# Raw weights in half tiles, another DMA rate in the planner, and one pool for block inverses and attention values, in a two-layer hybrid trunk

## The chip, the cores and the metric

The kernel runs on one core of one Trainium2 chip. The metric is device time in microseconds (us) of one execution. Names used below: PE is TensorE (matmuls), PEld its weight loads, DVE is VectorE, ACT is ScalarE, POOL is GpSimd, SP is SyncE, whose queue issues nearly all DMAs.

## The reference, cut to what matters

The input x is 512 tokens by 1024 channels; all numbers are fp32. Head width is 128. Layer 0 mixes with four gated DeltaNet heads (short convolution, chunked delta rule with chunks of 64) and four block-sparse MoBA heads; layer 1 has eight forgetting-attention (FoX) heads. Each mixer is `(mix * silu(z)) @ w_out`. After each layer comes a gate from the residual stream times a projection of a per-layer embedding p (256 wide).

```python
def ab_mixer(hn, w_in, ...):
    proj = hn @ w_in                       # 1024 x 4104
    ...                                    # conv, silu, l2norm; delta rule; MoBA
    y = jnp.concatenate([from_heads(oa), from_heads(ob)], axis=-1) * jax.nn.silu(z)
    return y @ w_out

def fox_mixer(hn, w_in, forget_b, w_out):
    proj = hn @ w_in                       # 1024 x 4104
    ...                                    # causal softmax(q.k/sqrt(d) + c_t - c_s)
    return (from_heads(o) * jax.nn.silu(z)) @ w_out

def reference(x, p, ...):
    for i in range(DEPTH):
        j = i // 2
        hn = rmsnorm(x, norm_g[i])
        if i % 2 == 0: x = x + ab_mixer(hn, w_in_ab[j], ...)
        else:          x = x + fox_mixer(hn, w_in_c[j], ...)
        gate = jax.nn.sigmoid(rmsnorm(x, ple_norm_g[i]) @ w_ple_gate[i])
        x = x + gate * (p[i] @ w_ple_proj[i])
    return rmsnorm(x, final_g)
```

In the delta rule a unit lower-triangular system is solved in each chunk of 64 tokens: `sol = triangular_solve(eye + a_mat, rhs)`, with `u, w = sol[..., :dv], sol[..., dv:]`.

## The kernel before, in words

**Weights.** Every weight product is made of three matmuls: each fp32 weight chunk `raw` is split on the chip into `whi` (a copy in the matmul's type) and `wlo = raw - whi`; activations are split into `hhi`, `hlo` (or `yhi`, `ylo`) likewise; hi·hi, lo·hi and hi·lo are summed in PSUM. The class `Weights` (L445 on) does it for all of `w_in`, `w_out`, `w_ple_gate` and `w_ple_proj`. A piece is 1024 x 512 weights, 2 MB, in one SBUF tile `raw` of 16 KB in each partition; two DMAs of 1 MB fill it. There is one such tile: the pair of DMAs for the next piece is issued when the last split of this piece has read it. A piece has four chunks. A chunk made by `cols` is 128 columns over all eight row blocks, so it reads both halves of the piece; a chunk made by `rows` is two row blocks of 512 columns and reads one half. Of split chunks there are three slots each (`whi`, `wlo`). A split is one copy of 128x1024 (`whi`, on ACT or DVE) and one subtraction of 128x1024 (`wlo`, on DVE or POOL). In the product `u` a chunk feeds 24 matmuls of 128x512; `vr` is the same with the weights as the moving side.

**The order.** A planner (`Plan`, L123 to L325) runs when the kernel is built. It keeps a clock for every engine, gives each operation a cost, and writes one fixed order of instructions for each engine and for the DMA queue of SP. It puts an operation next where its inputs are ready by its own clocks. All operations pass L186, so each row of the profile has that line; tiles tell them apart. A DMA's time in it is set on L177, by bytes:

```python
self.bw = max(end + 0.7, self.bw) + max(b / 1e6 * 2.8, ...) ...
```

The hardware then follows the written order: each engine takes its instructions one after the other, and waits in front of the one whose inputs aren't there, whatever stands behind it. Where the planner's own clock has PE waiting for 0.2 us, it puts a matmul named `idle` in PE's order (`until`, L291), which computes nothing that is used.

**Tiles.** `t2` has 55 slots of 2 KB in each partition, `t4` four of 4 KB. Two further tiles of 8 KB, `bd`, hold first the projection weights of the first embedding (`ple0`) and gate weights, later the inverses of the 64x64 blocks (`bds`) of the delta rule, one tile for the inverse and one for its transpose, each for all four heads. The inverses are worked out on DVE (`inverses`, L1156), written to DRAM (`xd`) and read back in block-diagonal form by eight DMAs of 64 KB on SP; the flag `bds` then lets `wy` (L1188) go on, which reads `wq` from DRAM and gives PE the products `t`, `w` and `u` of each head. Loads of weights are held from the start of the inverses' last part until these eight DMAs are issued (`Wait` in `loads`).

**Attention.** For 128 queries: `S` on PE, bias, maximum and exponent on DVE and ACT (`P`), transposes on PE (`PTp`), split into `PThi`, `PTlo` on ACT and DVE, and `O` on PE. In the FoX layer these stand in the engines' orders among the weight splits of the products beside them. FoX values are split into `vhi`, `vlo`.

## Time and profile before

| | |
|---|---|
| median of 3 runs | 742.52 us (739.96 to 742.71) |
| the profiled execution | 739.63 us, of which its span is 737.9 |
| PE busy | 702.7 us, 95% of the span, 3374 matmuls |
| DVE, ACT, POOL busy | 474.7, 341.1, 279.8 us (64, 46, 38%) |
| mean granted clock of PE | 0.986 |
| HBM read, written | 68.53 MB, 11.30 MB; 108 GB/s over the span |

A matmul's recorded time is longer than its share of PE: matmuls overlap, and their ends are modelled, so PE's time is best counted from start to start. The timeline has 96 matmuls `u` of 128x512 in a row in 22.10 us, 0.230 us each. Idle time in front of an instruction is shown with what ended it; the view of the waits sums it by engine and by what was waited for. The granted clock of a window (PEclk) is near 1.00 at 2.4 GHz and near 0.50 at 1.2 GHz. A transfer of DMA is read from its issue on SP's queue to the first instruction that waited for it.

### The profile page before, as it was taken

The page shows a single profiled execution, that of the slowest core. Times are in us where ns is not written, and L with a number is a line of the kernel's source. Part 1 is how long each engine was busy: PE and PEld are TensorE (multiplying, and loading weights), DVE is VectorE, ACT ScalarE, POOL GpSimd, SP SyncE. Part 2 cuts the span into 40 slices and gives each one's busy share as a digit, 9 for nine tenths or more (in the row PEclk, how much of TensorE's full clock was granted, in tenths as well). Part 3 has the DMA queues.
Part 4 walks back from the last instruction along what each step waited for, and adds up shares of the span by engine and source line. Part 5 has one row for each costly group of instructions (what it writes and reads, how often), then busy time and mean ns, then how long its engine had stood idle before and what let it go on. Part 6 is the DMA issues. An engine that isn't in the chain of part 4 may idle for free.

```text
span 737.9 us, 9199 instructions
## 1 busy us (share of the span) xinstructions
PE 702.7 (95%) x3374; PEld 577.9 (78%) x3374; DVE 474.7 (64%) x805; ACT 341.1 (46%) x634; POOL 279.8 (38%) x222
## 2 busy tenths in 40 slices
PE   7999988999999999999998999989999799999995
PEld 4887876888788787778886888868888688888884
DVE  3768864966665678776896443546337466776684
ACT  4638842225774364634553422345224463433545
POOL 3435554426551223025322344342336322535320
PEclk9999999999999999999999999989999999999998
DMA  7752424443424023143554035310453203244303
GB/s 257 261 144 78 152 73 128 143 114 90 111 58 115 2 69 116 25 165 125 200 185 125 17 116 141 96 49 1 114 143 100 72 1 138 79 170 157 114 1 114
DMA packets 51782, 80.41 MB, mean 109 GB/s; under 512 B 11133, under 2 KB 14542, under 8 KB 51738
## 3 DMA queue, kind: packets, MB, share of 16 engines
q1 hardware_dynamic: 51064, 78.74, 34.5%
q10 hardware_dynamic: 674, 1.09, 0.5%
q8 instruction: 26, 0.43, 0.2%
q14 instruction: 18, 0.15, 0.1%
HBM read 68.53 MB, written 11.30 MB: 108 GB/s over the span
## 4 chain that ended last, share of the span: by engine, by line
PE 69%; DMA 13%; DVE 9%; ACT 3%; POOL 3%; issue 2%; SPq 1%; ACTq 0%; DVEq 0%; POOLq 0%
PE u L186 40%; PE vr L186 8%; DMA raw<-in_w_in_c_dram 6%; DMA raw<-in_w_in_ab_dram 4%; PE O L186 3%; PE pp L186 3%; PE fg L186 3%; POOL wlo L186 2%; PE S L186 2%; ACT whi L186 2%; PE PTp L186 2%; DVE gt L186 1%; DVE wlo L186 1%; DMA bd<-in_w_ple_proj_dram 1%; PE su L186 1%
## 5 line engine op out<-in xcount | busy, mean ns | idle before, releaser
L186 POOL TENSOR_TENSOR wlo<-raw,whi 128x1024 fp32r<-128x1024 f32 x74 | 186.5, 2526 | 360.0 <-ACT whi L186 280.6
L186 PE MATMUL u<-hhi,whi 128*128 128x512 f32 x480 | 190.7, 397 | 3.2 <-ACT whi L186 3.1
L186 PE MATMUL u<-hlo,whi 128*128 128x512 f32 x480 | 190.2, 396 | 0.0
L186 PE MATMUL u<-hhi,wlo 128*128 128x512 f32 x480 | 163.1, 397 | 0.1
L186 ACT ACTIVATE whi<-raw 128x1024 fp32r<-128x1024 f32 x84 | 87.3, 1054 | 117.7 <-DMA raw<-in_w_in_c_dram 49.5
L186 PEld LDWEIGHTS u<-hhi,whi 128*128 128x128 f32 x480 | 90.3, 188 | 22.1 <-ACT whi L186 3.5
L186 PEld LDWEIGHTS u<-hhi,wlo 128*128 128x128 f32 x480 | 89.7, 188 | 18.4 <-POOL wlo L186 0.6
L186 PEld LDWEIGHTS u<-hlo,whi 128*128 128x128 f32 x480 | 90.3, 188 | 17.3
L186 DVE TENSOR_TENSOR wlo<-raw,whi 128x1024 fp32r<-128x1024 f32 x20 | 36.9, 1844 | 24.8 <-ACT whi L186 24.8
L186 PE MATMUL u<-yhi,whi 128*128 128x512 f32 x128 | 50.2, 392 | 1.4 <-ACT whi L186 1.4
L186 PE MATMUL vr<-wlo,hhi 128*128 128x512 f32 x128 | 51.4, 401 | 0.0
L186 PE MATMUL vr<-whi,hlo 128*128 128x512 f32 x128 | 51.3, 401 | 0.0
L186 PE MATMUL vr<-whi,hhi 128*128 128x512 f32 x128 | 51.3, 401 | 0.0
L186 PE MATMUL u<-ylo,whi 128*128 128x512 f32 x128 | 50.0, 391 | 0.0
L186 ACT ACT_TABLE_LOAD x33 | 42.3, 1283 | 2.1 <-DVE cacc L186 0.8
L186 PE MATMUL u<-yhi,wlo 128*128 128x512 f32 x128 | 42.4, 391 | 0.7 <-POOL wlo L186 0.7
L186 ACT ACTIVATE hhi<-xres,vec 128x512 fp32r<-128x512 f32 x24 | 17.3, 724 | 44.1 <-DVE xres L186 44.0
L186 ACT ACTIVATE P<-P,nmx 128x128 f32<-128x128 f32 (+3 forms) x48 | 26.7, 557 | 12.6 <-DVE nmx L186 11.7
L186 DVE SCALAR_TENSOR_TENSOR cacc<-u,vec,cacc 128x509 f32<-128x509 f32 (+2 forms) x36 | 26.7, 744 | 7.0 <-ACT cacc L186 6.4
L186 PEld LDWEIGHTS u<-yhi,whi 128*128 128x128 f32 x128 | 24.1, 188 | 6.7 <-ACT whi L186 1.9
L186 PEld LDWEIGHTS u<-yhi,wlo 128*128 128x128 f32 x128 | 24.0, 188 | 6.0 <-POOL wlo L186 1.1
L186 PEld LDWEIGHTS vr<-whi,hlo 128*128 128x128 f32 x128 | 24.6, 193 | 4.9
(299 smaller groups left out, 1277.8 us busy)
## 6 DMA issues: line engine op xcount, KB each, us to landing
raw<-in_w_in_ab_dram SPq DMA_DIRECT2D x16, 1024.0 KB, 9.7
raw<-in_w_in_c_dram SPq DMA_DIRECT2D x16, 1024.0 KB, 7.0
raw<-in_w_ple_gate_dram SPq DMA_DIRECT2D x8, 1024.0 KB, 5.0
raw<-in_w_out_ab_dram SPq DMA_DIRECT2D x4, 1024.0 KB, 7.2
raw<-in_w_out_c_dram SPq DMA_DIRECT2D x4, 1024.0 KB, 6.5
xr<-in_x_dram SPq DMA_DIRECT2D x8, 256.0 KB, 5.6
x0d<-x SPq DMA_DIRECT2D x8, 256.0 KB, 8.0
ppd<-ppt SPq DMA_DIRECT2D x8, 256.0 KB, 4.1
```

Of the source, the lines that this page charges most:

```text
L186: return op.f(*op.a, **op.k)
```

## The change

The tile of 16 KB for raw weights becomes three of 8 KB, each half of a piece, with its own slot, DMA and release. A half is loaded as soon as a slot is free, so that the first half of the next piece can be loaded while the piece before it is still being split. A `cols` chunk, which reads both halves, is split by two copies and two subtractions of 128x512; a `rows` chunk reads one half, and keeps one copy and one subtraction of 128x1024. In the planner, the cost of a DMA goes from 2.8 us for each MB to 5.2 for `w_in` and 3.4 for the rest. The two tiles of 8 KB go, `t4` has eight slots rather than four and `t2` 51 rather than 55. The block inverses are four tiles of 4 KB, for two heads each, filled by 16 DMAs of half the size (128x the same partitions, half the rows), the second pair of tiles only after the inversion; `wy` of heads 0 and 1 waits for the first pair alone (`bds0`). The first embedding's weights are two tiles of `t4`, `vhi`/`vlo` share one, and MoBA's values lie in two. Some tiles near the end are given back earlier.

```diff
@@ -174,7 +174,7 @@
             o = op.outs[0] if op.outs[0].space != bass.MemoryType.DRAM else op.ins[0]
             b = o.nbytes if not callable(o.nbytes) else o.nbytes()
             small = any(n.startswith(("kd", "ub", "xd", "graw", "vrow", "bd_", "qd", "gd", "Gb")) for n in op.w + op.r)
-            self.bw = max(end + 0.7, self.bw) + max(b / 1e6 * 2.8, 0.6 if small else 0.2) + 1.5 * ("graw" in op.w[0])
+            self.bw = max(end + 0.7, self.bw) + max(b / 1e6 * (5.2 if any("w_in" in n for n in op.r) else 3.4), 0.6 if small else 0.2) + 1.5 * ("graw" in op.w[0])
             end = self.bw + 0.9
         if op.locks():
             self.lock = end
...
@@ -322,7 +322,7 @@
         self.until(lambda: not any(g[4] for g in gs), "finish")
-NB2, NBH = 55, 16
+NB2, NBH = 51, 16
 PI = -1.6
...
@@ -353,8 +353,8 @@
         return (wp if pool in ("raw", "whi", "wlo") else gp).tile(shape, dt, name=nm(name), tag=f"{pool}_{i}", bufs=1)
     plan = Plan(make)
-    for pool, n in (("A", 4), ("B", 4), ("t2", NB2), ("th", NBH), ("t4", 4),
-                    ("raw", 1), ("whi", 3), ("wlo", 3)):
+    for pool, n in (("A", 4), ("B", 4), ("t2", NB2), ("th", NBH), ("t4", 8),
+                    ("raw", 3), ("whi", 3), ("wlo", 3)):
         plan.pools(pool, n)
     V, A, G, T, SP = (Eng(k, o) for k, o in (("DVE", nc.vector), ("ACT", nc.scalar), ("POOL", nc.gpsimd),
                                             ("PE", nc.tensor), ("SP", nc.sync)))
...
@@ -393,12 +393,10 @@
-    bd = [gp.tile([P, GH * NT * P], F32, name=nm("bd"), tag="bd", bufs=2)]
-    ple0 = bd[0].rearrange("p (k c) -> p k c", k=2)
+    ple0 = [plan.take("t4", "ple", (P, 2, 512)) for _ in range(2)]
-        do(A.dma_start(ple0[:, :, c * 512:(c + 1) * 512],
-                       w_ple_proj[0, :, c * 512:(c + 1) * 512].rearrange("(k q) c -> q k c", q=P)))
+        do(A.dma_start(ple0[c], w_ple_proj[0, :, c * 512:(c + 1) * 512].rearrange("(k q) c -> q k c", q=P)))
...
@@ -437,10 +435,7 @@
-    def gst_tile():
-        return gp.tile([P, GH * NT, P], F32R, name=nm("gst"), tag="bd", bufs=2)[:, 0:KT, :]
-
-    gst0 = gst_tile()
+    gst0 = plan.take("t4", "gst", (P, KT, P), F32R)
...
@@ -460,15 +455,17 @@
         def cols(self, w, c0):
-            self.add(self.views(w, c0), [(lambda r, j=j: r[:, :, j * P:(j + 1) * P], (KT, P)) for j in range(4)])
+            self.add(self.views(w, c0), [([(h, slice(None), slice(j * P, (j + 1) * P), slice(4 * h, 4 * h + 4)) for h in range(2)],
+                                          (KT, P)) for j in range(4)])
         def rows(self, w, c0):
-            self.add(self.views(w, c0), [(lambda r, j=j: r[:, 2 * j:2 * j + 2, :], (2, 512)) for j in range(4)])
+            self.add(self.views(w, c0), [([(j // 2, slice(2 * (j % 2), 2 * (j % 2) + 2), slice(None), slice(None))], (2, 512))
+                                         for j in range(4)])
         def ple(self, w):
             self.add([w[:, c * 512:(c + 1) * 512].rearrange("(k q) c -> q k c", q=P) for c in range(2)],
-                     [(lambda r, c=c: r[:, 2 * c:2 * c + 2, :], (2, 512)) for c in range(2)])
+                     [([(c, slice(0, 2), slice(None), slice(None))], (2, 512)) for c in range(2)])
         def add(self, views, parts):
             self.pieces.append(views)
...
@@ -480,28 +477,31 @@
                 if views is None:
                     self.loaded.append(ple0)
                     continue
-
-                yield Wait(lambda: "inv3" not in flags or "bds" in flags)
-                raw = yield Slot("raw", "raw", (P, KT, 512))
-                n = views[0].shape[1]
-                for k, view in enumerate(views):
-                    yield SP.dma_start(raw[:, k * n:(k + 1) * n], view)
-                self.loaded.append(raw)
+                self.loaded.append([])
+                for view in views:
+
+                    yield Wait(lambda: "inv3" not in flags or "bds" in flags)
+                    raw = yield Slot("raw", "raw", (P, 4, 512))
+                    yield SP.dma_start(raw[:, 0:view.shape[1]], view)
+                    self.loaded[i].append(raw)
         def splits(self):
-            for i, (piece, f, (a, c)) in enumerate(self.chunks):
-                yield Wait(lambda: len(self.loaded) > piece)
-                raw = f(self.loaded[piece])
+            for i, (piece, parts, (a, c)) in enumerate(self.chunks):
+                yield Wait(lambda: len(self.loaded) > piece and len(self.loaded[piece]) == 2)
+                halves = self.loaded[piece]
                 hi = yield Slot("whi", "whi", (P, a, c), F32R)
                 lo = yield Slot("wlo", "wlo", (P, a, c), F32R)
                 far = i - self.used >= 1
-                yield copy(hi, raw, 0.8)
-                w = [V.tensor_tensor(out=lo, in0=raw, in1=hi.bitcast(F32), op=ALU.subtract),
-                     G.tensor_tensor(out=lo, in0=raw, in1=hi.bitcast(F32), op=ALU.subtract)]
-                yield Any((w[0], 2.5 if far else 0.0), w[1])
+                for h, k, w, o in parts:
+                    yield copy(hi[:, o, :], halves[h][:, k, w], 0.8)
+                for h, k, w, o in parts:
+                    ops = [e.tensor_tensor(out=lo[:, o, :], in0=halves[h][:, k, w], in1=hi[:, o, :].bitcast(F32),
+                                           op=ALU.subtract) for e in (V, G)]
+                    yield Any((ops[0], 2.5 if far else 0.0), ops[1])
                 self.split.append((hi, lo))
-                if piece and (i + 1 == len(self.chunks) or self.chunks[i + 1][0] != piece):
-                    free(raw)
+                rest = {x[0] for q in self.chunks[i + 1:] if q[0] == piece for x in q[1]}
+                for h in {x[0] for x in parts} - rest:
+                    free(halves[h])
                 self.urge()
         def urge(self):
...
@@ -1179,10 +1179,14 @@
         yield V.tensor_copy(vbT, vb.rearrange("p a b -> p b a"))
         yield SP.dma_start(xd[1].rearrange("b h t r c -> (b h t) r c"), vbT)
         drop(vb, vbT)
-        for k in (0, 1):
-            for bl in range(4):
-                yield SP.dma_start(bds[k][bl * 32:(bl + 1) * 32, :, bl * 32:(bl + 1) * 32],
-                                   xd[k, bl].rearrange("h t r c -> r (h t) c"))
+        flags.add("inverted")
+        for h0 in range(2):
+            yield Wait(lambda: len(bds) >= 2 * h0 + 2)
+            for k in (0, 1):
+                for bl in range(4):
+                    yield SP.dma_start(bds[2 * h0 + k][bl * 32:(bl + 1) * 32, :, bl * 32:(bl + 1) * 32],
+                                       xd[k, bl, 2 * h0:2 * h0 + 2].rearrange("h t r c -> r (h t) c"))
+            flags.add(f"bds{h0}")
         flags.add("bds")
     def wy(hh):
...
@@ -1194,10 +1198,10 @@
         yield G.tensor_tensor(out=kdc, in0=kr, in1=b3(eGLG, hh), op=ALU.mult)
         yield G.tensor_tensor(out=kr, in0=kr, in1=b3(eGp, hh), op=ALU.mult)
-        yield flag("bds")
+        yield flag(f"bds{hh // 2}")
         wq = yield Slot("t4", "wq", (P, NT, 4, 64))
         yield SP.dma_start(wq[:, :, 1:3, :], qd[hh].rearrange("p (t c i) -> p t c i", c=2, i=64))
-        bdT, bd = (b[:, hh * NT:(hh + 1) * NT, :] for b in bds)
+        bdT, bd = (b[:, hh % 2 * NT:(hh % 2 + 1) * NT, :] for b in bds[hh // 2 * 2:hh // 2 * 2 + 2])
         ps = yield Slot("B", "t1", (P, NT, P))
         for t in range(NT):
             yield T.matmul(ps[:, t, :], lhsT=kn[hh][:, t * P:(t + 1) * P], rhs=bd[:, t, :], start=True, stop=True)
...
@@ -1310,10 +1316,13 @@
     bds = []
     def blocks():
+
         yield flag("gates")
-        for k in range(2):
-            bds.append(gp.tile([P, GH * NT, P], F32, name=nm("bd"), tag="bd", bufs=2))
-            yield G.memset(bds[k], 0.0)
+        for k in range(4):
+            yield flag("inv" if k < 2 else "inverted")
+            b = yield Slot("t4", "bd", (P, 2 * NT, P))
+            yield G.memset(b, 0.0)
+            bds.append(b)
     def delta():
         run(scales(), -1)
...
@@ -1360,11 +1370,12 @@
-            v = (None, t2("vhi", F32R), t2("vlo", F32R))
+            pair = yield Slot("t4", "vhl", (P, 2, S), F32R)
+            v = (None, pair[:, 0, :], pair[:, 1, :])
-            v = (t2("vb"),)
+            v = (t2("vb") if key else vpair[t // 2][:, t % 2, :],)
...
@@ -1414,6 +1425,7 @@
+    vpair = [plan.slot("t4", "vp", (P, 2, S)) for _ in range(2)]
...
@@ -1627,10 +1639,12 @@
             yield SP.dma_start(fgt, final_g[c * 512:(c + 1) * 512].unsqueeze(0).to_broadcast([P, 512]))
             yield G.tensor_scalar(out=fgt, in0=fgt, scalar1=-0.5, scalar2=None, op0=ALU.mult)
             fg.append(fgt)
-        yield Wait(lambda: len(W.loaded) == len(W.pieces))
-        raw = yield Slot("raw", "raw", (P, KT, 512))
-        for kc, view in enumerate(W.views(w_ple_gate[1], 512)):
-            yield SP.dma_start(raw[:, kc * 4:(kc + 1) * 4], view)
+        yield Wait(lambda: len(W.loaded) == len(W.pieces) and len(W.loaded[-1]) == 2)
+        raws = []
+        for view in W.views(w_ple_gate[1], 512):
+            raw = yield Slot("raw", "raw", (P, 4, 512))
+            yield SP.dma_start(raw, view)
+            raws.append(raw)
         for kc in range(2):
             for k in range(4):
                 if kc:
...
```

The planner writes a new order from this. In all PE has the same products; its `idle` matmuls go from 50 to 53. The 84 copies `whi<-raw` of 128x1024 on ACT become 18 of 128x1024 and 127 of 128x512; the 74 subtractions `wlo<-raw,whi` of 128x1024 on POOL become 17 and 134, and the 20 on DVE become 1 and 18. SP has 162 rows rather than 135.

SP's queue in the FoX layer before: `raw` are weight tiles (x2: two DMAs of 1 MB), `biasc` the attention's bias rows.

```order
L186 DMA raw_3879<-in_w_in_c_dram 128x4x512 x2
L186 DMA biasc_3969<-cd 128x512
L186 DMA biasc_3971<-cd 128x512
L186 DMA raw_4039<-in_w_in_c_dram 128x4x512 x2
L186 DMA biasc_4192<-cd 128x512
L186 DMA biasc_4258<-cd 128x512
```

The same stretch of SP's queue now, each `raw` a half:

```order
L186 DMA raw_4006<-in_w_in_c_dram 128x4x512
L186 DMA raw_4018<-in_w_in_c_dram 128x4x512
L186 DMA raw_4088<-in_w_in_c_dram 128x4x512
L186 DMA biasc_4103<-cd 128x512
L186 DMA biasc_4105<-cd 128x512
L186 DMA raw_4164<-in_w_in_c_dram 128x4x512
L186 DMA biasc_4345<-cd 128x512
L186 DMA biasc_4411<-cd 128x512
```

The pairs have become single DMAs, with one half (`raw_4018`) issued before the slot of the other (`raw_4088`) is free.

ACT in the FoX layer before, at the first chunk of the piece `raw_4039`: `P` are rows of attention weights, `PThi` the split of their transposes, which `O` on PE needs.

```order
L186 ACTIVATE P_4060<-P_4060,rs_4096 128x384
L186 ACTIVATE whi_4101<-raw_4039 128x1024
L186 ACTIVATE P_4111,sums_4063<-P_4111,nmx_4062 128x512
L186 ACTIVATE PThi_4144<-PTp_4140 128x384
L186 ACTIVATE PThi_4155<-PTp_4152 128x256
```

The same place of ACT's order now:

```order
L186 ACTIVATE P_4259,sums_4197<-P_4259,nmx_4196 128x512
L186 ACTIVATE whi_4285<-raw_4018 128x512
L186 ACTIVATE PThi_4298<-PTp_4294 128x384
L186 ACTIVATE PThi_4309<-PTp_4306 128x256
L186 ACTIVATE P_4236<-P_4236,rs_4279 128x384
L186 ACTIVATE PT_4320<-PTp_4318 128x128
L186 ACTIVATE oT_4334<-O_4323 128x512
L186 ACTIVATE whi_4285<-raw_4088 128x512
```

The copy from the half loaded early stands ahead of the `PThi`, and the copy from the late half stands six instructions further down. Further on, where before had `whi_4869<-raw_4802` ahead of `PThi_4899`, three `PThi`/`PT` and an `oT` now stand ahead of the copy from the late half in the same way.

PE before, between the two pieces of layer 0's `w_out` (`yhi`, `ylo` are the split mix, `whi_2873` the first chunk of the second piece; nine `idle` in all):

```order
L186 MATMUL u_2867<-yhi_2819,wlo_2849 128x512
L186 MATMUL idle_2915<-onesr 128x512
L186 MATMUL idle_2921<-onesr 128x512
...
L186 MATMUL idle_2940<-onesr 128x512
L186 MATMUL u_2946<-yhi_2453,whi_2873 128x512
```

PE now, at the same place:

```order
L186 MATMUL u_2985<-yhi_2891,wlo_2941 128x512
L186 MATMUL u_2985<-yhi_2913,wlo_2941 128x512
L186 MATMUL u_3030<-yhi_2597,whi_2962 128x512
L186 MATMUL u_3030<-ylo_2598,whi_2962 128x512
```

The `idle` matmuls are gone there. Counted over the whole order, nine go here, three a little earlier in layer 0's `w_out`, six in the FoX layer at the chunk `whi_4869`, and one ahead of a chunk in layer 0; where before had three ahead of the chunk `whi_1145` of `w_in`, there are now four. Eight come in ahead of the first `u` of the program and in the embedding product before it, seven ahead of a chunk of the last `w_ple_gate`, four ahead of the first product `t` of the delta rule, and one each at two chunks.

## Rows read from the trace of the kernel before

**Rows 1.** The page: engine, busy us, share of the span, instructions

```profile
PE 702.7 (95%) x3374; PEld 577.9 (78%) x3374; DVE 474.7 (64%) x805; ACT 341.1 (46%) x634; POOL 279.8 (38%) x222
```

**Rows 2.** Waits of PE: for what; us in total, times, longest

```profile
PE u L186 <- ACT whi L186: 4.5, 2, 3.1
PE O L186 <- DVE PTlo L186: 4.3, 1, 4.3
PE O L186 <- ACT PThi L186: 3.6, 1, 3.6
PE ssps L186 <- ACT sshi L186: 3.1, 1, 3.1
```

**Rows 3.** Windows: us, busy of PE, PEld, DVE, ACT, POOL, then PEclk, DMA

```profile
396.00:399.40 3.40, 3.40 (x9) 2.72 (x9) 1.17 (x2) 2.69 (x4) 2.36 (x1) 0.50 0.00 0
484.60:491.50 6.90, 5.78 (x20) 4.96 (x21) 4.28 (x8) 2.37 (x7) 6.43 (x11) 0.51 0.01 2
576.80:580.30 3.50, 3.24 (x11) 2.97 (x11) 3.41 (x9) 0.62 (x4) 3.50 (x6) 0.51 0.02 5
```

**Rows 4.** Timeline of PE near 117: start us, us, instruction, [idle before <-releaser]

```profile
117.06 0.86 PE L186 MATMUL idle<-onesr 128*128 128x512 f32 x3
120.99 0.51 PE L186 MATMUL u<-hhi,whi 128*128 128x512 f32 x1 [3.08 <-ACT whi L186]
```

**Rows 5.** Chain that ended last: start us, us, what

```profile
120.99 22.10 PE u L186 x96
```

**Rows 6.** Timeline of PE between the pieces of w_out

```profile
316.01 2.23 PE L186 MATMUL idle<-onesr 128*128 128x512 f32 x9
319.68 0.50 PE L186 MATMUL u<-yhi,whi 128*128 128x512 f32 x1 [1.44 <-ACT whi L186]
```

**Rows 7.** Timeline of PE near 482

```profile
485.72 0.69 PE L186 MATMUL O<-PThi,vhi 128*128 128x384 f32 x1 [3.57 <-ACT PThi L186]
```

**Rows 8.** Timeline of ACT near 482

```profile
483.39 1.06 ACT L186 ACTIVATE whi<-raw 128x1024 fp32r<-128x1024 f32 x1 [7.09 <-DMA raw<-in_w_in_c_dram]
...
485.18 0.77 ACT L186 ACTIVATE PThi<-PTp 128x384 fp32r<-128x384 f32 x2
```

**Rows 9.** Timeline of PE near 572

```profile
577.06 0.80 PE L186 MATMUL O<-PThi,vhi 128*128 128x512 f32 x1 [4.26 <-DVE PTlo L186]
```

**Rows 10.** Timeline of ACT near 572

```profile
574.74 1.06 ACT L186 ACTIVATE whi<-raw 128x1024 fp32r<-128x1024 f32 x1 [5.22 <-DMA raw<-in_w_in_c_dram]
575.70 0.58 ACT L186 ACTIVATE PThi<-PTp 128x512 fp32r<-128x512 f32 x1
```

**Rows 11.** Timeline of SP's queue: issues of raw pairs and of bd

```profile
108.14 0.94 SPq L186 DMA_DIRECT2D raw<-in_w_in_ab_dram  x2
...
178.45 12.94 SPq L186 DMA_DIRECT2D bd<-xd  x8
...
469.16 0.93 SPq L186 DMA_DIRECT2D raw<-in_w_in_c_dram  x2
...
561.62 0.94 SPq L186 DMA_DIRECT2D raw<-in_w_in_c_dram  x2
```

**Rows 12.** Timeline of PE: the first product t of the delta rule

```profile
195.97 1.95 PE L186 MATMUL t<-bd,kn 128*128 128x128 f32 x16
```

**Rows 13.** Lines by form: instruction xcount | busy us, mean ns | idle before

```profile
L186 POOL TENSOR_TENSOR wlo<-raw,whi 128x1024 fp32r<-128x1024 f32 x74 | 186.5, 2526 | 360.0 <-ACT whi L186 280.6 <-DVE whi L186 25.3 <-PE vr L186 13.9
...
L186 ACT ACTIVATE qhi<-q 128x512 fp32r<-128x512 f32 x14 | 8.8, 629 | 24.3 <-DVE q L186 24.3
...
L186 POOL TENSOR_TENSOR decay<-Gb,gmask 128x512 f32<-128x512 f32 x4 | 5.2, 1288 | 0.0
```

**Rows 14.** Timeline of DVE ahead of ssps

```profile
388.22 0.68 DVE L186 TENSOR_TENSOR gt<-u,rstd 128x512 f32<-128x512 f32 x1
...
389.60 2.70 DVE L186 TENSOR_TENSOR gt<-gt,ppr 128x512 f32<-128x512 f32 x1
```

**Rows 15.** Timeline of POOL at that time

```profile
388.81 2.93 POOL L186 TENSOR_TENSOR wlo<-raw,whi 128x1024 fp32r<-128x1024 f32 x1 [4.18 <-ACT whi L186]
```

More of the change, by code (lines that the diff above doesn't have):

```diff
@@ L535 @@
     W = Weights()
-    W.add(None, [(lambda r, c=c: r[:, :, c * 512:(c + 1) * 512], (2, 512)) for c in range(2)])
+    W.add(None, [([(c, slice(0, 2), slice(None), slice(None))], (2, 512)) for c in range(2)])
     B0 = 1544
@@ L570, in later_loads @@
     def later_loads():
-        yield Wait(lambda: len(W.loaded) > 1)
+        yield Wait(lambda: len(W.loaded) > 1 and len(W.loaded[1]) == 2)
         yield load_gate("ab", w_in_ab[0], 1536)
@@ L1229, in wy @@
         us[hh], wqs[hh], kds[hh] = u, wq, kdc
+        if hh // 2 * 2 in us and hh // 2 * 2 + 1 in us:
+            drop(*bds[hh // 2 * 2:hh // 2 * 2 + 2])
     def scan(hs):
@@ L1352 @@
     run(gates(gate_unit(st["gst"], h)), -1)
+    drop(gst0)
     delta()
@@ L1425, in after @@
         drop(*tiles())
-    run(after(gens, lambda: [v[0] for v in vrows.values()]), 0)
+    run(after(gens, lambda: vpair), 0)
     def gating(zs, order, oT, y, g):
@@ L1580 @@
         attend(qk, heads, lambda hh, i: (vrows2[hh // 4][i], slice((hh % 4) * P, (hh % 4 + 1) * P)), bias_c, oTc, 0.2, gens)
-        run(after(gens[4 * half:], lambda half=half: [a for v in vrows2[half].values() for a in v if a is not None]), 0)
+        run(after(gens[4 * half:], lambda half=half: [v[-1] for v in vrows2[half].values()]), 0)
     pT = []
@@ L1642, in late @@
                     hi, lo = a[:, k % 2, :], b[:, k % 2, :]
-                yield copy(hi, raw[:, kc * 4 + k])
-                yield minus(lo, raw[:, kc * 4 + k], hi.bitcast(F32), 0.0)
+                yield copy(hi, raws[kc][:, k])
+                yield minus(lo, raws[kc][:, k], hi.bitcast(F32), 0.0)
                 gw[kc * 4 + k] = (hi, lo)
     run(late(), -0.5)
+    turned = [0, 0]
     def gate_row(t, c, ps, ss, a, b, gt, before=None):
@@ L1662, in gate_row @@
         yield V.tensor_tensor(out=gt[:, w], in0=gt[:, w], in1=ppr[c * 4 + t][:, w], op=ALU.mult)
+        if b == 512:
+            drop(ppr[c * 4 + t])
+            turned[c] += 1
+            if turned[c] == NT:
+                drop(*x3[c * 4:c * 4 + 4])
         yield V.tensor_tensor(out=gt[:, w], in0=gt[:, w], in1=xps[:, w], op=ALU.add)
```

## The prediction

> **What bounds the kernel now.** I read the page's busy times first [rows 1]: PE is at 95% of the span, with ACT at 46% and POOL at 38%. So the products set the time, and a change that leaves PE's products alone can move only what PE does not do: waits, `idle` matmuls, and half-speed stretches. Then I read the waits of PE [rows 2]. The reader is to see that the large ones, 3.1 to 4.3 us each, end on a split or on an attention tile, not on a product. Third come the windows of the granted clock [rows 3]: after a wait of 3 us or more PE runs for 3.4 to 6.9 us at 0.50 or 0.51, the 1.2 GHz level, so each such wait is paid again. About half of a stretch is lost: 1.7 us of 3.4 or 3.5, 3.4 of 6.9. The timelines last [rows 4, 6 to 10], to see what stood in front of each wait.
>
> All are one mechanism. There is one raw tile, so the next piece's two DMAs are issued when the last split of this piece is done. From issue to the first copy it takes 108.14 to 119.88, 11.7 us (the copy's start is PE's 120.99 less its 1.06, with 0.05 between); 469.16 to 483.39, 14.2 us; 561.62 to 574.74, 13.1 us [rows 4, 8, 10, 11]. PE has three split chunks to live on and falls short by 3 to 4 us. In the FoX layer it is worse: the `whi` copy stands on ACT ahead of `PThi`, so `O`, which needs nothing of the new piece, waits until the copy has its data. ACT sat idle 7.09 and 5.22 us there; `PThi` came behind the copy at 485.18 and 575.70, and PE's `O` 0.5 and 1.4 us later [rows 7 to 10].
>
> **The change part by part.** The sum is made against the profiled execution, 739.63 us; the median of the runs shown is 2.9 us above it.
>
> *Halves.* The first half of a piece can be on its way while the piece before it is split; only the second is issued when a slot comes free. It has half the bytes: by the three times above, 5.9 to 7.1 us of waiting in place of 11.7 to 14.2. So data are there 5.9 to 7.1 us sooner, more than any of the waits at issue. From the other side, if what is between issue and landing did not shrink with bytes, nothing would be gained; I take the value by bytes, since the first half is out of the wait altogether.
> - Near 117: from the first `idle` at 117.06 to `u` at 120.99 PE does nothing useful for 3.93 us [rows 4]. The order now has four `idle` there. One costs 0.230 us, since 96 matmuls `u` of the same shape take 22.10 [rows 5], so four cost 0.92. Gain 3.0.
> - Between the pieces of `w_out`: 316.01 to 319.68, 3.67 us [rows 6], with no `idle` there now, and three fewer a little earlier, 0.7. Gain 4.4.
> - Near 482: the wait of 3.57 [rows 7] and half of 6.9 at half speed [rows 3]. In the order the copy ahead of `PThi` is now the one from the early half; the late one stands behind. Gain 3.6 + 3.4 = 7.0.
> - Near 572: 4.26 [rows 9], 1.7 of clock [rows 3], and six `idle`, 1.4. Gain 7.4.
>
> Together 21.8 us. The wait for `sshi` (3.1 and 1.7 of clock) I leave as it is: it ends on DVE, as a rival below says.
>
> *The rate in the planner.* With 5.2 us for each MB of `w_in` (a pair of 2 MB then 10.4, near the 11.7 to 14.2 above) the planner no longer counts on data that aren't there. That is what moves ACT's late copies behind `PThi`. It has a price: where it now sees PE waiting, it writes `idle`. Eight more at the start, seven at the last gate's weights, four ahead of `t`, two elsewhere: 21 x 0.230 = 4.8 us, less one that goes, 0.2. I take 4.6. They would cost nothing where PE would have waited anyway, which is so in part at the start; below that, 2.8 without the eight.
>
> *More instructions.* On ACT 66 of the 84 large copies give way to 127 small. A copy of 128x1024 has 1.06 [rows 8], one of 128x512 on ACT 0.629 [rows 13]: 127 x 0.629 - 66 x 1.06 = 9.9 us more. On POOL, 57 of the large go and 134 small come: with 1.288 for a subtraction-like instruction of 128x512 and 2.526 for the large [rows 13], 172.6 - 144.0 = 28.6 us more, of which 25.3 are ten chunks that moved over from DVE (20 to 10). ACT would go from 46 to 48% and POOL from 38 to 42%; both stay covered by PE's 95%. Behind the landing the first subtraction may start after 0.63, where it was 1.06, and the chunk ends after 0.63 + 2 x 1.29 = 3.2 rather than 1.06 + 2.4. So nothing for it; if the cover were gone, each first chunk after a wait would cost the 0.2 us of its second copy.
>
> A rule of the Trainium skill speaks against this part. By "Perfetto Trace Analysis", section "Optimizing Scalar/DVE Operations", each ScalarE instruction on SBUF carries about 93 ns of its own, and larger operations are better where an engine is saturated. By that figure 61 more copies are an estimated 6 us of ACT; the rows give 9.9. In the sum both are nothing, with ACT at 46%; only if ACT held PE up at every piece would it show.
>
> *Block inverses and pools.* The eight issues of `bd` held SP for 12.94 us from 178.45, and the first `t` started at 195.97, 4.6 us after their end [rows 11, 12]. Sixteen of half the size move as many bytes; heads 0 and 1 need eight. So `t` could start earlier, but it is placed earlier too, some 4 us by the work ahead of it. I take nothing; bounds -4 and +5, with a clock stretch of 3.4 on top.
>
> *New waits.* An order written anew has its own misjudged places. None can be seen in the trace of before. From below nothing; from above as much as the four now, 21.8. I take one: 3.5 (the mean of those in rows 2 that went longest) and a stretch of clock between 1.7 and 3.4, 6.0 together.
>
> Sum: -21.8 + 4.6 + 6.0 = -11.2 us, so 728.4 for a profiled execution and 731.3 for the median: 1.5% less.
>
> **The rivals.**
> *Waits only change place.* Total bytes and the number of 1 MB DMAs are as before, and the second half of a `w_in` piece still can't be issued until the last `cols` chunk has let both halves go. If its landing still decides in half of the places, 11 us of the 21.8 go back, and with 4.6 and 6.0 the sum is about zero: 742. For it: all four waits stand behind a transfer issued late. Against: 5.9 us saved exceeds 4.3, the longest.
>
> *Slower, by the block inverses.* Sixteen issues behind one another on SP, the second eight after a memset on POOL, and the `wq` loads and the next `raw` behind them. One issue of `bd` took 12.94 / 8 = 1.6 us. If an issue of half the size takes as long, sixteen take 26 us, 13 more than before; `w`, `u` of all heads and the raw loads held behind the flag come 13 us later. PE has other products there but lives on three chunks: a wait of 13 and 3.4 of clock on top of the main sum make 731.3 + 16.4 = 747.7. It decides from the point where `wq` of heads 0 and 1 is issued later than some 20 us after the first `bd`. Against: the inversion ends no later, and half the rows should take about half.
>
> *More gained, by shorter instructions on POOL.* DVE's `gt<-gt,ppr` took 2.70 us at 389.60, its like 0.68 a moment before, while POOL was in a `wlo` from 388.81 to 391.74 [rows 14, 15]: DVE ended where it would have by starting after POOL. `ssps` at 395 then waited 3.1 [rows 2], with 1.7 of clock [rows 3]. With `wlo` in halves of 1.29, DVE can be held at most 1.3 rather than the 2.0 here, and the wait falls under what starts a half-speed stretch: 4 us more, 727. The Trainium skill, "SBUF — State Buffer", section "SBUF: two separate sides", says that DVE and GpSimd share a port pair as a lock held for a whole instruction; the row agrees (2.70 against 0.68). Against: twice as many POOL instructions may hold DVE twice as often.
>
> **How the numbers follow.** The main case has 0.50, more gained 0.17, waits that change place 0.19, slower 0.14. The main case alone spans 725 to 738: new waits from nothing (-6) to 12.7. The range to 746 takes in the rival of no change and part of the slower one; below it goes to 720, no new waits and the `ssps` wait gone as well. 0.5% of 742.52 is 3.7 us, about what a measurement of this kernel can tell from no change. Faster: 0.50 less a tenth, 0.17, and a fifth of the third case, 0.70. Same: most of the third and a little of the main case, 0.16. Slower: 0.14.
>
> **What would show it.** In the profile of the changed kernel: the row of `u` behind `whi` near 117 and the `O` near 482 and 572 without waits of 3 us; ACT's waits for raw of `w_in_c` well under their 5 to 7 us each; PEclk at 1.00 in these places; no wait at `t`; PE's busy time as before but a span of about 727. Wrong: waits of 3 us or more for `whi`, `PThi` or `t` at new places with stretches of half speed, or the `bd` issues taking over 20 us.

## The result and the profile after

The changed kernel takes 717.14 us (median of 4 runs, 715.61 to 717.30) against 742.62 us for the kernel before in the same comparison (739.96 to 744.93): the ratio is 0.9653, 95% interval 0.9619 to 0.9688, 25.5 us less. The forecast was 731.3, range 720 to 746: the direction and the four places that it named were right, the size was less than half of what came.

The profiled execution took 717.13 us, with a span of 715.3 and a granted clock of 0.994. The page's busy times of the kernel after, to set beside [rows 1]:

```profile
PE 696.8 (97%) x3377; PEld 574.9 (80%) x3377; DVE 461.0 (64%) x829; ACT 344.0 (48%) x684; POOL 323.1 (45%) x303
```

PE's share is 97% and its matmuls are three more. ACT grew by 2.9 us, not 9.9: its 61 more weight copies took 6.0 us more, and 16 squares fewer stand on it. POOL grew by 43.3, not 28.6. Neither bounds the kernel, with PE at 97%. The waits of PE, after (for what; us in total, times, longest), to set beside [rows 2]:

```profile
PE ssps L186 <- ACT sshi L186: 2.5, 1, 2.5
PE idle L186 <- DVE onesr L186: 2.0, 1, 2.0
PE idle L186 <- ACT sqr L186: 1.7, 1, 1.7
PE vr L186 <- DVE gt L186: 1.0, 1, 1.0
```

No row for `u` behind `whi` is left, and none for `O`. The one large wait that stays is `ssps`. The waits of ACT's copies for `w_in` before:

```profile
ACT whi L186 <- DMA raw<-in_w_in_c_dram: 49.5, 8, 9.6
ACT whi L186 <- DMA raw<-in_w_in_ab_dram: 24.3, 4, 12.8
```

The waits of ACT's copies, after:

```profile
ACT whi L186 <- PE u L186: 69.2, 29, 3.3
...
ACT whi L186 <- PE vr L186: 25.6, 7, 4.8
...
ACT whi L186 <- DMA raw<-in_w_in_c_dram: 3.6, 2, 2.0
```

The reader is to see what the copies wait for now: PE, which frees the slots of split chunks, 94.8 us in all, and a transfer of `w_in` for 3.6 us only, where it was 73.8. Splitting keeps ahead of PE. The four places, after: PE's timeline near 114, between the pieces of `w_out`, and at the FoX tile that answers to [rows 7].

```profile
114.50 1.09 PE L186 MATMUL idle<-onesr 128*128 128x512 f32 x4
115.43 0.40 PE L186 MATMUL u<-hhi,whi 128*128 128x512 f32 x1
...
310.14 0.39 PE L186 MATMUL u<-yhi,whi 128*128 128x512 f32 x1
...
475.74 0.51 PE L186 MATMUL O<-PThi,vhl 128*128 128x384 f32 x2
```

The four `idle` are there, and nothing is waited for behind them; no wait is in brackets at any of the three. ACT at the last of these places:

```profile
473.29 0.49 ACT L186 ACTIVATE PThi<-PTp 128x384 fp32r<-128x384 f32 x1 [0.91 <-PE PTp L186]
474.20 0.39 ACT L186 ACTIVATE PThi<-PTp 128x256 fp32r<-128x256 f32 x1 [0.42 <-PE PTp L186]
...
477.60 0.62 ACT L186 ACTIVATE whi<-raw 128x512 fp32r<-128x512 f32 x1
```

`PThi` waits 0.9 us for PE's transposes, and the copy from the late half runs behind, at 477.60, without a wait. Windows of the clock, after (PEclk is the third number from the end), to set beside [rows 3]:

```profile
383.00:391.00 8.00, 5.54 (x17) 4.14 (x17) 5.46 (x9) 4.90 (x6) 2.37 (x1) 0.79 0.17 49
466.00:480.00 14.00, 14.00 (x77) 11.70 (x76) 8.37 (x23) 7.05 (x18) 6.59 (x10) 1.00 0.08 29
552.00:564.00 12.00, 12.00 (x72) 10.35 (x71) 7.61 (x19) 5.40 (x13) 5.76 (x11) 1.00 0.41 139
```

The FoX layer is at 1.00 in both windows, and over 395 to 680 us as a whole. The stretch behind `ssps` is the one left: 0.79 over 8 us, so some 3.4 us at the 1.2 GHz level. In another execution of the same kernel (e11 below) `ssps` waits the same 2.5 us, but PEclk is 1.00 in these 8 us and the span is 1.5 us shorter.

From the timelines of both executions, start times of the same product give where the time went. The last column is the prediction's term for that stretch.

| up to | before | after | change in the stretch | predicted |
|---|---|---|---|---|
| `u` after its 48th hi·hi | 71.74 | 72.28 | +0.5 | +1.8 |
| `u` near 117 | 120.99 | 115.43 | -6.1 | -3.0 |
| first `u` of `w_out` | 291.10 | 286.56 | +1.0 | +0.9 |
| second piece of `w_out` | 319.68 | 310.14 | -5.0 | -4.4 |
| FoX values, `vr` | 461.02 | 451.39 | -0.1 | 0 |
| `u` behind the first FoX heads | 531.40 | 515.30 | -6.5 | -7.0 |
| second embedding product | 624.80 | 600.76 | -7.9 | -7.4 |
| last product `fg` | 703.58 | 681.20 | +1.7 | +1.6 |
| sum | | | -22.4 | -17.5 |

The prediction's own sum was -11.2: these terms, 0.3 elsewhere, and the 6.0 of new waits.

### The profile page after: what moved, and what is told of

Read it like the earlier page. It is cut to its first block, busy times and chain, and to the rows that moved or that the text cites. A ratio compares the mean times of both kernels' runs of the same rounds, so it can differ in the third digit from the quotient of the medians.

```text
span 715.3 us, 9412 instructions
## 1 busy us (share of the span) xinstructions
PE 696.8 (97%) x3377; PEld 574.9 (80%) x3377; DVE 461.0 (64%) x829; ACT 344.0 (48%) x684; POOL 323.1 (45%) x303
## 4 chain that ended last, share of the span: by engine, by line
PE 89%; DVE 6%; ACT 2%; issue 1%; DMA 1%; POOL 1%; DVEq 0%; ACTq 0%
PE u L186 54%; PE vr L186 12%; PE O L186 3%; PE S L186 3%; PE fg L186 3%; PE pp L186 3%; PE PTp L186 2%; DVE gt L186 2%; PE idle L186 1%; DVE sq L186 1%; PE su L186 1%; PE t L186 1%; PE ws L186 1%; DMA prow<-in_p_dram 1%; DVE xres L186 1%
## 5 line engine op out<-in xcount | busy, mean ns | idle before, releaser
L186 POOL TENSOR_TENSOR wlo<-raw,whi 128x512 fp32r<-128x512 f32 (+1 forms) x151 | 230.7, 1539 | 279.0 <-ACT whi L186 207.2
L186 ACT ACTIVATE whi<-raw 128x512 fp32r<-128x512 f32 (+1 forms) x145 | 93.3, 676 | 104.6 <-PE u L186 69.2
L186 DVE TENSOR_TENSOR wlo<-raw,whi 128x512 fp32r<-128x512 f32 (+1 forms) x19 | 22.0, 1185 | 13.9 <-ACT whi L186 13.9
L186 PEld LDWEIGHTS vr<-whi,hhi 128*128 128x128 f32 x128 | 24.3, 190 | 6.3 <-DVE gt L186 1.4
L186 PEld LDWEIGHTS vr<-wlo,hhi 128*128 128x128 f32 x128 | 24.3, 190 | 4.8
```

The costliest lines, as they stand in the source:

```text
L186: return op.f(*op.a, **op.k)
```

## The experiments

Two theories stood first: that a half loaded ahead brings the gain (A), and that the honest DMA rate in the planner brings it (B). Each kernel is compared with the kernel before, on the same chip.

**The rate alone.** The kernel before, with

```diff
-... + max(b / 1e6 * 2.8, 0.6 if small else 0.2) ...
+... + max(b / 1e6 * (5.2 if any("w_in" in n for n in op.r) else 3.4), 0.6 if small else 0.2) ...
```

> The kernel before with only the planner's DMA rate changed (5.2 us for each MB of w_in, 3.4 for the rest); raw weights stay one tile of 16 KB. In its order PE has 119 idle matmuls, where before had 50. Theory A, that the gain is data landing sooner because a half is loaded ahead: the planner now counts the waits honestly but can't remove them, so the waits for raw become idle matmuls. 69 more at 0.230 us are 16 us, against about 17 us of waits and half-speed stretches that go (the four weight waits, 13 us, and their clock, 5); about 738 us, between 732 and 745. Theory B, that the gain is the honest rate (copies of late data no longer stand ahead of PThi): most of the 25 us is here, about 722 us.

Measured: 745.12 us, ratio 1.0017 (0.9992 to 1.0041). No gain, so B falls; it is also 7 us above A's 738. PE's `idle` in it (count, duration ns min/median/max, first and last start):

```profile
L186 PE MATMUL idle<-onesr x119: 388/393/792, 1.9 to 731.7; 128*128 128x512 f32 x119
```

119 of them, 27 us: the rate alone tells the planner of waits and turns them into `idle` matmuls, and the time is the same.

**The halves with the old rate.** The changed kernel with 2.8 for all weights.

```diff
-(5.2 if any("w_in" in n for n in op.r) else 3.4)
+2.8
```

> The changed kernel with the planner's DMA rate put back to 2.8 us for each MB for all weights; halves and pools stay. PE has 42 idle matmuls. Theory A: most of the gain stays, since halves land in time whatever the planner believes; 718 to 724 us, with perhaps one wait of 3 us in the FoX layer where a copy stands ahead of PThi. Theory B: the waits of before come back at other places, 734 to 742 us.

Measured: 715.25 us, 0.9609 (0.9589 to 0.9629). All of the gain is there, a little more than A's range had.

**Two half slots rather than three.**

```diff
-("raw", 3), ("whi", 3), ("wlo", 3)
+("raw", 2), ("whi", 3), ("wlo", 3)
```

> The changed kernel with two slots of 8 KB for raw halves rather than three: every edit stays but no half can be loaded ahead, for a cols piece both halves are freed together by its last chunk. PE has 88 idle matmuls, 35 more than with three slots, 8 us. Theory A (the third slot is what gains): about 733 to 740 us, with ACT's waits for raw of w_in back at 4 us or more each. A rival, that releasing each half by itself is enough: within 3 us of the changed kernel and its idle matmuls, 717 to 726 us.

Measured: 727.03 us, 0.9761 (0.9738 to 0.9785), between the two numbers expected. It has 88 `idle`:

```profile
L186 PE MATMUL idle<-onesr x88: 388/393/796, 2.0 to 713.2; 128*128 128x512 f32 x88
```

**Small instructions, no half tiles.** The kernel before, one raw tile of 16 KB, with a `cols` chunk split by two copies and two subtractions:

```diff
-yield copy(hi, raw, 0.8)
+for o in cuts:                     # row blocks 0 to 3, then 4 to 7
+    yield copy(hi[:, o, :], raw[:, o, :], 0.8)
 ...                                # likewise the subtraction lo = raw - hi
```

> The kernel before with only the split of a cols chunk cut into two copies and two subtractions of 128x512 (one raw tile, old rate, old pools). If the wait of 2.8 us at kq and the 3.1 us at ssps come from DVE held by POOL's 2.4 us subtractions, shorter ones take 2 to 5 us off: 736 to 741 us, with DVE's small instructions near 85 to 95 us no longer at 1.8 to 2.4 us. If the size of the instructions has nothing to do with the gain: 742 to 746 us, with more instructions on ACT and POOL and all waits for raw as before.

Measured: 715.54 us, 0.9612 (0.9591 to 0.9633). Neither expectation foresaw it: the whole gain with one raw tile, the old rate and the old pools. This overthrows A in the form in which the prediction had it, that the first half must be loaded ahead. Its timeline near 115 (SP's queue, ACT and PE):

```profile
107.79 0.95 SPq L186 DMA_DIRECT2D raw<-in_w_in_ab_dram  x2
...
114.35 2.23 PE L186 MATMUL idle<-onesr 128*128 128x512 f32 x9
...
115.04 0.62 ACT L186 ACTIVATE whi<-raw 128x512 fp32r<-128x512 f32 x1
...
116.42 0.39 PE L186 MATMUL u<-hhi,whi 128*128 128x512 f32 x1
...
119.15 1.15 ACT L186 ACTIVATE whi<-raw 128x512 fp32r<-128x512 f32 x2 [3.48 <-DMA raw<-in_w_in_ab_dram]
...
119.83 0.50 PE L186 MATMUL u<-hhi,whi 128*128 128x512 f32 x1 [1.41 <-ACT whi L186]
```

The pair is issued at 107.79. The first copy starts 7.25 us later, long before the second, so with what one of the two DMAs brought, and PE, behind nine `idle`, begins the chunk at 116.42 with what that copy wrote; the second copy starts at 119.15, and PE waits for it only 1.41 us. In [rows 4, 11] copy and PE stood still for both. So a theory L: a copy waits for the transfers that wrote what it reads, and a half copy waits for one. At this place the gain is small: at the next chunk e4 is 3.0 us ahead of the kernel before (123.59 against 126.60), and the wait of 2.8 us for `kq`, further up, is gone too.

**The two edits of that kernel apart.** Copies in halves only, and subtractions in halves only (same `cuts`).

> The kernel before with only the copies whi of a cols chunk cut in two (128x512 each); subtractions stay 128x1024, one raw tile, old rate. After e4 took 28 us off with no half tile at all, two theories. Theory L, landing: a copy of 128x512 reads what one DMA of 1 MB brought, so the first no longer waits for the second; then the copies alone carry most, 717 to 726 us. Theory S, size of the subtraction: POOL's 2.4 us subtraction delays the release of the raw tile, the chunk and DVE; then the copies alone change little, 736 to 744 us.

> The kernel before with only the subtractions wlo of a cols chunk cut in two (128x512 each, on DVE or POOL); copies stay 128x1024, one raw tile, old rate. Theory L: the copies still wait for both DMAs, so the waits near 117, 482 and 572 stay; 734 to 743 us. Theory S: most of the 28 us, 716 to 726 us.

Measured: copies alone 729.13 us, 0.9808 (0.9780 to 0.9837); subtractions alone 731.38 us, 0.9842 (0.9804 to 0.9880). Each lies between the ranges of the two theories and is under half of e4's gain, so neither is enough; together they add up to 24.0 of its 28.4 us. Copies alone leave a wait of 3.1 us for `O`; ACT ahead of it in that kernel:

```profile
560.16 0.63 ACT L186 ACTIVATE whi<-raw 128x512 fp32r<-128x512 f32 x1 [1.49 <-DMA raw<-in_w_in_c_dram]
563.68 0.63 ACT L186 ACTIVATE whi<-raw 128x512 fp32r<-128x512 f32 x1 [2.89 <-DMA raw<-in_w_in_c_dram]
564.22 0.58 ACT L186 ACTIVATE PThi<-PTp 128x512 fp32r<-128x512 f32 x1
```

The second half's copy stands ahead of `PThi` here, waits 2.89 us, and `PThi` with it: the written order decides whether a late half hurts. With the subtractions cut alone, the waits for raw stay (waits of PE):

```profile
PE u L186 <- ACT whi L186: 5.0, 3, 2.8
PE PTp L186 <- ACT P L186: 3.5, 2, 3.3
PE O L186 <- DVE PTlo L186: 2.7, 1, 2.7
```

By start times its gain came mostly at `ssps` (5.1 us between 385 and 417), where it no longer waits. That is not by shorter subtractions: the chunks split there are `rows` chunks, which this edit leaves at 128x1024, and DVE's instructions there still take up to 2.92 us. That points to the new order.

**One DMA for both halves.** e4 with one transfer of 2 MB for each piece; the written order of each engine is the same, instruction for instruction.

```diff
-return [w[k * 512:(k + 1) * 512, c0:c0 + 512]... for k in range(2)]
+return [w[0:1024, c0:c0 + 512].rearrange("(k q) c -> q k c", q=P)]
```

> e4 (the kernel before with copies and subtractions of 128x512) with each piece of 2 MB loaded by one DMA in place of two; the order of every engine is instruction for instruction that of e4, so only the landing differs. Theory L: the first copy must wait for all 2 MB, some 3 to 5 us longer at each w_in piece; ACT's waits for raw grow from 43 us to over 60, and PE gets waits of 2 to 4 us back: 722 to 735 us. Theory S (and a third, that the new order alone matters): within 2 us of e4's 715.5.

Measured: 742.46 us (737.16 to 754.14), 0.9985 (0.9958 to 1.0012). Some 27 us are gone, though only the landing differs, and theory L's range, which ended at 735, is passed. The profiled execution took 748.23 us, more than the median, so its rows are read for the mechanism, not for sizes. Its timeline at the place shown for e4:

```profile
109.91 0.40 SPq L186 DMA_DIRECT2D raw<-in_w_in_ab_dram  x1
...
117.16 2.23 PE L186 MATMUL idle<-onesr 128*128 128x512 f32 x9
...
121.13 1.15 ACT L186 ACTIVATE whi<-raw 128x512 fp32r<-128x512 f32 x2 [3.17 <-DMA raw<-in_w_in_ab_dram]
...
121.82 0.50 PE L186 MATMUL u<-hhi,whi 128*128 128x512 f32 x1 [2.43 <-ACT whi L186]
```

The first copy comes 11.22 us behind the issue, as in the kernel before, and behind the same nine `idle` PE waits 2.43 us before it can begin the chunk at all. But much of what e7 loses is not at `cols` chunks. The `rows` chunks of the values read one half of a piece in the kernel before and in e4; here they, too, wait for all 2 MB. ACT at the first such piece in e4, then in e7, and two waits of PE in e7 that neither e4 nor the kernel before has:

```profile
135.16 2.00 ACT L186 ACTIVATE whi<-raw 128x1024 fp32r<-128x1024 f32 x2
```

```profile
144.91 2.00 ACT L186 ACTIVATE whi<-raw 128x1024 fp32r<-128x1024 f32 x2 [5.83 <-DMA raw<-in_w_in_ab_dram]
```

```profile
PE vr L186 <- ACT whi L186: 5.2, 3, 2.7
PE vr L186 <- POOL wlo L186: 4.7, 3, 1.7
```

These are 9.9 us, at three places, and at each of them a half-speed stretch follows (PEclk 0.50 over 148.5 to 151.9, 397.7 to 401.1 and 476.2 to 483.0), some 6.8 us more: about half of the 32.3 us by which the profiled execution of e7 is longer than that of e4. And not all that e4 gained is lost. Between the pieces of `w_out` e7 keeps 4.4 us against the kernel before where e4 has 4.7, and at the place of [rows 7] `O` waits 0.3 us at most: at these two places the smaller instructions and their order remove the wait without the landing. Near 117 and near 572 e7 loses 2.4 and 4.1 us of e4's gain. So both count, the landing of 1 MB rather than 2 in front of a copy, and an order that keeps late copies out of the way, which e5 shows too. That e7 ends at the time of the kernel before is partly chance; what the landing is worth at the `cols` chunks alone, no run shows.

**Two half slots and the old rate.** e2 and e3 together.

> The changed kernel with two half slots (no half loaded ahead) and the old rate of 2.8: e3 without the 43 idle matmuls that the honest rate adds (88 there, 45 here). If the third slot gains nothing by itself and e3 was slow by its idle matmuls: 727.0 less 43 x 0.230 = 9.9, so 715 to 719 us. If the third slot is what removes the waits: they come back without the idles that stood for them, 725 to 735 us.

Measured: 713.95 us, 0.9604 (0.9577 to 0.9632), a little under the first range. With the old rate the third slot gains nothing: e2, which has it, took 715.25. The waits of ACT's copies in it:

```profile
ACT whi L186 <- DMA raw<-in_w_in_c_dram: 28.5, 11, 6.1
ACT whi L186 <- DMA raw<-in_w_in_ab_dram: 25.1, 7, 8.9
```

ACT again waits 53.6 us for `w_in`, as against 3.6 in the changed kernel and 11.3 in e2, and PE waits for none of it. So the third slot shortens only waits that cost nothing. With the new rate it is different: e3, with two slots, took 9.9 us more than the changed kernel. What makes e3 slow is most likely its `idle` matmuls: 43 more than here are 9.9 us at 0.230, and the difference is 13.1. At 121.0 us e3 has 19 of them in a row, 4.50 us, at the chunk for which e8 has one and PE doesn't wait.

**No `idle` matmuls.** The changed kernel without them.

```diff
-if self.warm is not None and asleep >= 0.2 and ...
+if self.warm is not None and asleep >= 1e9 and ...
```

> The changed kernel with no idle matmuls in PE's order (53 there; all products stay). The prediction booked 4.6 us for those that the change adds. If an idle matmul costs its time: 53 x 0.230 = 12.2 us less, less what PE must wait for anyway at the start and the end (some 7 us), so 709 to 713 us. If they only fill waits that PE would have, and keep its clock: the same time or longer by the half-speed stretches that come back behind the waits, 716 to 724 us.

Measured: 720.27 us, 0.9657 (0.9617 to 0.9696), 4.1 us more than the changed kernel on that chip (e11). The waits and the clock that they had covered (waits of PE; then 180 to 195 us of e9):

```profile
PE pT L186 <- DMA prow<-in_p_dram: 7.0, 1, 7.0
PE tr L186 <- ACT cacc L186: 3.9, 2, 2.6
```

```profile
180.00:195.00 15.00, 11.09 (x51) 7.70 (x49) 10.21 (x22) 14.14 (x22) 10.74 (x10) 0.89 0.45 92
```

PEclk is 0.89 there; the changed kernel has 1.00 in the same window. In sum the 53 `idle` matmuls of the changed kernel pay for themselves. That doesn't go for `idle` matmuls as such: those of e3 most likely cost it time.

**`rows` chunks in halves too,** on top of e8:

```diff
-[(j // 2, slice(2 * (j % 2), 2 * (j % 2) + 2), slice(None), slice(None))]
+[(j // 2, slice(2 * (j % 2) + m, 2 * (j % 2) + m + 1), slice(None), slice(m, m + 1)) for m in range(2)]
```

> e8 (two half slots, old rate) with the rows chunks, too, split by two copies and two subtractions of 128x512. POOL's longest subtraction is then 1.3 us, where e8 still has ones of 2.4 in the gate products. If DVE held by POOL makes the wait at ssps (2.8 us in e8, with a half-speed stretch behind it): gt<-gt,ppr falls from some 1.5 us to 1.0, the wait by 0.5 to 2.8 us and the time by up to 4: 710 to 713 us. If that wait is DVE's own chain: 713 to 716 us, with 8 idle matmuls more in its order.

Measured: 715.93 us, 0.9600 (0.9560 to 0.9640). The mechanism is as the first expectation has it, the time isn't. The timeline ahead of `ssps` in e8 (POOL and DVE), then that of DVE in e10:

```profile
380.67 2.77 POOL L186 TENSOR_TENSOR wlo<-raw,whi 128x1024 fp32r<-128x1024 f32 x1 [2.61 <-DVE whi L186]
...
381.12 2.88 DVE L186 TENSOR_TENSOR gt<-gt,ppr 128x512 f32<-128x512 f32 x1
```

```profile
382.03 0.69 DVE L186 TENSOR_TENSOR gt<-gt,ppr 128x512 f32<-128x512 f32 x1 [0.70 <-ACT gt L186]
```

In e8 DVE's 0.69 us became 2.88, ending 0.56 us after POOL's subtraction, a little less than its own length; in e10 it is 0.69, and the wait for `sshi` fell from 2.8 to 1.2 us. There was no half-speed stretch to win back, though the expectation has one: PEclk is 1.00 in e8 from 383 to 392 us. By start times e10 gains 1.6 us around `ssps` and loses 3.9 between the pieces of `w_out`, where its order has nine `idle` rather than two.

**The changed kernel and e8 side by side.**

> The changed kernel itself, for a comparison on one chip with e8 (next). 717 us.

> e8 again (the changed kernel with two half slots and the old rate), beside the changed kernel on one chip. If the third slot and the new rate gain nothing, it is faster than the changed kernel by its fewer idle matmuls, 8 x 0.230 = 1.8 us, or a little more: 713 to 716 us. If they do gain: slower than the changed kernel.

Measured: 716.13 us (715.56 to 717.05) and 714.57 us (712.18 to 716.04), 6 runs each. e8 is 1.6 us faster by medians, and the two sets overlap. So two slots and the old rate are at least as good; that they are better isn't shown beyond doubt.

## Why the prediction was wrong

Read step by step:

- *What bounds it.* Right: PE's products stayed, and the waits that stand behind raw weights and the clock behind them went. The four gains were booked at 21.8 us; the stretches with them gave 5.0, 6.5, 7.9, and near 117 6.1 with the wait that the next point but one names.
- *The step that failed* is "New waits": "I take one: ... 6.0 together". It is the largest part of the miss, and no wait of that kind came: what is new in front of PE is 1.7 us at the start (`sqr`), 1.0 and 0.8, with no half-speed stretch at a new place. Why none came stays open. That the splits now wait for PE, so that there is something in hand, fits the changed kernel, and e2, where a rate that is off by half gives 715.25 all the same. But in e8 ACT waits 53.6 us for transfers, and PE waits for none of them. The end "from below nothing" was the better value, since no row of the kernel before showed a place for one.
- *A wait left out.* `kq` waited for `kn` near 95 in the kernel before, and the prediction put it at nothing without a word:

```profile
PE kq L186 <- DVE kn L186: 2.8, 1, 2.8
```

It is gone: 3.1 us more than forecast up to 117. e5 and e4 have none there either, with large and with small subtractions, so it isn't POOL's size alone; what in the order removes it stays open.
- *`idle` matmuls.* Of the 4.6 us booked, those at the start came out at 0.5 rather than 1.8; the others were right, at the last gate's weights (+1.7) and ahead of `t` (+1.0). That they cost anything in sum isn't borne out: without all 53, old and new, the kernel takes 4.1 us more.
- *From the profiled execution to the median.* 2.9 us were added since before's profiled execution was under its median. After's was at its median, 717.13 and 717.14. With 6.0, 3.1, 1.3 and 2.9 the miss of 14.2 us is accounted for but for about 1.
- *What the halves do.* This step failed too, without a price in the sum. "The first half is out of the wait altogether" names the half loaded ahead, which needs the third slot. With the old rate that slot is worth nothing (e8), and e4 gains all without half tiles: what counts is that an instruction reads one transfer's data, and the order that the planner makes of the smaller instructions. *The rate*, which the text had moving the copies behind `PThi`, gains nothing either (e1, e2). That the four terms came out right does not speak for this picture: they were read from what PE lost at each place, and any edit that removes these waits yields them.
- *The clock.* "After a wait of 3 us or more PE runs for 3.4 to 6.9 us at 0.50 or 0.51" is so at three places, but not near 117: behind the wait of 3.08 us there PEclk is 1.00 from 121 to 125 us. The sum did not use it there.
- *Rivals.* Waits didn't change place. The block inverses didn't hold the kernel up; the timeline after of SP's queue and PE, against [rows 11, 12]:

```profile
175.35 9.16 SPq L186 DMA_DIRECT2D bd<-xd  x16
...
188.03 1.17 PE L186 MATMUL t<-bd,kn 128*128 128x128 f32 x9
```

Sixteen issues took 9.16 us, where eight of twice the size took 12.94. The 1.6 us for an issue, on which that rival rests, were not its usual price; eight of the full size in e4, with no raw transfer issued just ahead:

```profile
168.11 4.13 SPq L186 DMA_DIRECT2D bd<-xd  x8
```

The flag for the first pair alone does nothing: a kernel in which all heads wait for both pairs has the same written order on every engine. Shorter POOL instructions do shorten the hold on DVE (e10), but the changed kernel kept `ssps` at 2.5 us: in its gate products the subtractions are still 128x1024, and two of DVE's `gt<-gt,ppr` ahead of `ssps` took 1.53 and 1.49 us. The 4 us of that rival didn't come there. The lock that the Trainium skill tells of in "SBUF — State Buffer", section "SBUF: two separate sides", is still seen at these instructions: in e8 one of them took 2.88 us against 0.69.

## What to carry to other kernels

Cut an instruction where its inputs were cut: when two transfers fill a tile, a reader of the whole tile waits for both, and its successors and whatever stands behind it on its engine wait too. Smaller instructions can also let the written order put the late half behind urgent work. Try that before buying buffer slots or tuning a planner's rates: here two loops in one function gave the whole gain. Don't book a new wait against a change without a place for it, and go through all waits of the trace, not only the largest four.

## What the runs showed that was not expected

- PE starts on a chunk that is split halfway: `u` at 116.42 in e4 reads the first half 0.76 us after its copy's end and 2.7 us before the second copy starts.
- The same kernel and the same wait, with and without a half-speed stretch behind it: in e8 and in its repeat, e12, `ssps` waits 2.8 us; PEclk is 1.00 from 383 to 392 us in e8 and 0.86 from 383 to 395 in e12. So a stretch at half speed, which costs some 1.7 us, may come or not from one execution to the next, and the 1.6 us between the medians of the changed kernel and e8 are no more than that.
- An issue on SP of `bd` took 1.62 us on average for the eight that came 0.6 us behind a pair of raw DMAs, 0.52 for the eight of the same size in e4, and 0.57 for the sixteen halves of the changed kernel. So the price goes with the transfer issued just ahead, not with the size.
